# One kind of PSUM bank, eight reads: ScalarE's four ahead of VectorE's four in a neighbourhood attention

## The chip, the cores and the metric

One core of a Trainium2 chip. The metric is the device time of one execution in microseconds, smaller is better; of several runs the median is given. A difference below about 0.2% (5.5 us here) can hardly be told from none.

## What is computed

A trunk of two layers over 1024 latent tokens (a grid of 16 rows by 64 columns) and 256 context tokens, width 1024, 16 heads of 64. Layer 0 mixes tokens with a 2-D neighbourhood attention (window 8 x 16, learned bias) in which each latent query also sees all context keys; layer 1 with a sliding window. Both layers end in a gated ConvFFN. All is float32.

```python
def attn_inputs(h, w_qkv, g_q, g_k, n_kv, with_q=True):
    y = h @ w_qkv
    q = rmsnorm(y[..., :D_MODEL].reshape(bsz, t, n_kv, N_HEADS // n_kv, HEAD_DIM), g_q)
    kv = y[..., D_MODEL:]
    k = rmsnorm(kv[..., :kv_w].reshape(bsz, t, n_kv, HEAD_DIM), g_k)
    v = kv[..., kv_w:].reshape(bsz, t, n_kv, HEAD_DIM)
    return q, k, v
...
for i in range(DEPTH):
    h = modulate(rmsnorm(x, g_attn[i]), sh1, sc1)
    hc = modulate(rmsnorm(ctx, g_attn[i]), sh1c, sc1c)
    q, k, v = attn_inputs(h, w_in, gq, gk, n_kv)
    q_c, k_c, v_c = attn_inputs(hc, w_in, gq, gk, n_kv, with_q=not last)
    o = neighbourhood_attention(q, k, v, k_c, v_c, na_rpb[j])     # i = 0
    x = x + gt1 * (o @ w_out)
    ...                                                           # context alike, then ConvFFN
```

## The kernel before

The program runs its stages one after the other on one core: an opening (modulation vectors, norm and first projections), the first attention, its output projection, the ConvFFN of layer 0, and the same for layer 1. Within a stage a planner, `Sched`, makes the order: every operation is entered with an engine (or a choice of engines), an assumed duration, a key, what it reads and writes, and the buffer slots that it takes (`acq`) and gives back (`rel`). `run` plays the engines against those durations; among the operations that could start, the lowest key goes first. Tables of small corrections to the keys, `KINDS` (by the operation's name) and `RANKS` (by its number), belong to each stage. The result is a fixed order of instructions on each engine, and each engine executes in order. The waits between engines (semaphores) come from the tiles that instructions share, whole PSUM banks included, and not from the planner. Every instruction is recorded by one helper, so all stand under one line, L51; one goes by the tiles' names.

The first attention is the stage `na`. It goes over 8 pairs of heads (`hp`) and, for each, over 10 tiles of 128 tokens (the two of the context first) in `plan_na_qkv`: three products per 128 of depth into a bank `mm` (float32 is split into a high and a low part: `whi`/`wlo` are the weights', `h0hi`/`h0lo`, `n1lo`, `h0chi`/`h0clo` the activations'); ScalarE copies it out to `qraw`, squares it (`sq`); VectorE sums (`qv`); GpSimd takes the power -0.5 (`qy`); VectorE refines that and scales to `qn`. The value part `v` gets its low half by a subtraction on GpSimd or VectorE.

After every second tile comes **the turn**: four transposes (`pt<-idr,qn`) put queries and keys of two tiles, for both heads of the pair, into one bank `pt`: columns 0 to 255 are queries, 256 to 511 keys; head 0 lies in partitions 0 to 63, head 1 in 64 to 127. There are 40 turns. From this bank are made, for each of the two heads (`h2`), with names as the profile has them:

- `qh` (ScalarE, `q<-pt,gg`): the query's high part, scaled;
- `ql` (VectorE, `q<-pt,gg,q`): its low part, into the other half of the partitions;
- `kh` (ScalarE, `kkl<-pt`, for the context `kkc<-pt`): the key's high part;
- `kx` (`kkl<-kkl` or `kkc<-kkc`): a copy of it into the other half of the partitions, between SBUF and SBUF;
- `kl` (VectorE, `kll<-pt,kkl`, or `klc`): the key's low part.

So a bank sees eight reads, four by ScalarE and four by VectorE. The tag `pt` has two banks in rotation, and they serve every transpose of the stage: the turns, the transposed probabilities (`pt<-idr,S`, whose high part is ScalarE's `pthi<-pt` and whose remainder VectorE's `pthi<-pt,pthi`), and a few others (`pt<-wm,cpad`: modulation products; `pt<-idr,rs`: sums of the softmax). Whoever allocates a bank waits for the last read of the user before the last.

The scores (`s<-kkc,q`, `klc`, `kkl`, `kll`) and what follows are `plan_su`: VectorE makes the negated scores with the bias and their minimum (`S`, `m`), ScalarE the exponential, TensorE transposes, and the weighted sums go to `pv`; ScalarE and VectorE bring them out (`pvup`, `osb`). In the last two pairs of heads the probabilities are scaled (`S<-S,sm`) on VectorE or ScalarE; in the others the output is (`odiv`).

Of the kernel before, what the change touches and what calls it, by code (L numbers as in the profile page):

```python
# [12 lines left out]
F32R = mybir.dt.float32r  # L13
# [4 lines left out]
P = 128  # L18
# [20 lines left out]
class InOrder:  # L39
# [7 lines left out]
    def __getattr__(self, name):  # L47
        f = getattr(self.eng, name)

        def call(*a, **k):  # L50
# [11 lines left out]
    open=dict(load=-0.7, mm=-6.4, cp=0.6, tr=-3.7, fin_=-5.6, sq=4, v=-2.5, newton=4.7, dg=2.3, bc=0.5, lof=-10.6,  # L62
          mod=-1.6),
    na=dict(eps=-3.7, f=0.3, cp=-1, sq=-2.5, vhi=10, vlo=2.9, ql=-11.4, kl=0.1, mm=-0.1, ctx_part=5.2, exp=1.3, hi=-0.5,
          lo=0.5, pvm=-1.3, add=-11.1, load=-1, lat_part=-0.5, rec=3.4, ev=0.1, scale=9.4),
# [8 lines left out]
    open={0: 0.9, 1: 54.2, 3: 50.3, 4: 23, 5: 10.7, 7: 0.6, 9: -44.5, 10: -12.7, 12: -32.6, 13: 65.9, 14: 53,  # L74
# [17 lines left out]
    na={36: 1, 40: 28.4, 42: 3, 46: 15.2, 61: 3.8, 64: -25, 67: 12.6, 69: -45.3, 71: -43.5, 74: 12.7, 81: -34.3,  # L92
# [309 lines left out]
def trunk_kernel(ctx, tc, xperm, xtok, xseq, cc, wmod0, wmod, bmod, gnorm, na_wqkv, na_gq, na_gk, na_bias, na_wo,  # L402
# [124 lines left out]
    def t_actp(n):  # L527
        return 0.051 + n / 1200.0
# [816 lines left out]
    def plan_na_qkv(n):  # L1345
# [1797 lines left out]
```

## Time and profile before

| | us |
|---|---|
| median of 3 runs (lowest, highest) | 2764.96 (2764.88, 2765.37) |
| the profiled execution | 2765.64 |
| its span in the profile | 2763.9 |
| busy in the span: TensorE / VectorE / ScalarE / GpSimd | 2708.3 / 2272.7 / 1685.4 / 381.2 |
| granted TensorE clock, mean over the span | 0.998 |

TensorE is busy for 98% of the span, and the chain of work that ended last lies on it for 73%. An average over stages hides what one stage waits for: the first attention, from about 70 to 743 us, is the one that the change touches, and the opening ahead of it is planned with tables that also change. Busy time of TensorE counts modelled ends of matmuls, which overlap; two products one behind the other start closer together than either lasts. Idle time below 0.15 us is the pipeline's own and not listed as a wait.

### The profile page before, as it was taken

The page shows a single profiled execution, that of the slowest core. Times are in us where ns is not written, and L with a number is a line of the kernel's source. Part 1 is how long each engine was busy: PE and PEld are TensorE (multiplying, and loading weights), DVE is VectorE, ACT ScalarE, POOL GpSimd, SP SyncE. Part 2 cuts the span into 40 slices and gives each one's busy share as a digit, 9 for nine tenths or more (in the row PEclk, how much of TensorE's full clock was granted, in tenths as well). Part 3 has the DMA queues.
Part 4 walks back from the last instruction along what each step waited for, and adds up shares of the span by engine and source line. Part 5 has one row for each costly group of instructions (what it writes and reads, how often), then busy time and mean ns, then how long its engine had stood idle before and what let it go on. Part 6 is the DMA issues. An engine that isn't in the chain of part 4 may idle for free.

```text
span 2763.9 us, 43693 instructions
## 1 busy us (share of the span) xinstructions
PE 2708.3 (98%) x15375; PEld 2379.5 (86%) x15375; DVE 2272.7 (82%) x4767; ACT 1685.4 (61%) x3220; POOL 381.2 (14%) x631
## 2 busy tenths in 40 slices
PE   7999999999999999999999999999999999999999
PEld 6888898888789997788888889999988888888887
DVE  5777788889869677789998699888896989888766
ACT  5777676778646554455554457888874655555443
POOL 1211111113100000000000005556440000000000
PEclk9999999999999999999999999999999999999999
DMA  7223233333745654444467562010264234334745
GB/s 284 67 90 120 87 99 126 109 107 108 248 149 181 189 168 144 157 153 152 154 213 262 157 215 81 13 35 19 72 188 154 73 115 145 122 107 148 255 149 190
DMA packets 153104, 387.29 MB, mean 140 GB/s; under 512 B 23356, under 2 KB 38708, under 8 KB 151476
## 3 DMA queue, kind: packets, MB, share of 16 engines
q1 hardware_dynamic: 152884, 384.50, 42.3%
q8 instruction: 121, 1.98, 0.3%
q14 instruction: 99, 0.81, 0.1%
HBM read 313.39 MB, written 71.04 MB: 139 GB/s over the span
## 4 chain that ended last, share of the span: by engine, by line
PE 73%; DVE 2%; ACT 2%; DMA 1%; issue 1%; POOL 0%; SPq 0%; DVEq 0%; POOLq 0%; ACTq 0%
PE ua L51 17%; PE dn L51 15%; PE uc L51 12%; PE mm L51 8%; PE ud L51 4%; PE oacc L51 4%; PE pt L51 3%; PE pv L51 3%; PE s L51 3%; PE dnc L51 2%; PE u L51 1%; ACT S L51 0%; PE mod L51 0%; ACT whi L51 0%; DVE S L51 0%
## 5 line engine op out<-in xcount | busy, mean ns | idle before, releaser
L51 ACT ACTIVATE whi<-wraw 128x512 fp32r<-128x512 f32 (+1 forms) x264 | 213.0, 808 | 180.8 <-PE uc L51 55.4
L51 DVE TENSOR_TENSOR wlo<-wraw,whi 128x512 fp32r<-128x512 f32 (+1 forms) x264 | 240.8, 914 | 39.9 <-ACT whi L51 39.4
L51 ACT ACTIVATE S<-S,m 128x640 f32<-128x640 f32 (+4 forms) x288 | 220.9, 768 | 50.3 <-DVE m L51 43.6
L51 PE MATMUL dn<-ghi,whi 128*128 128x512 f32 x616 | 239.9, 390 | 0.0
L51 PE MATMUL dn<-ghi,wlo 128*128 128x512 f32 x616 | 239.7, 389 | 0.0
L51 PE MATMUL dn<-glo,whi 128*128 128x512 f32 x616 | 239.6, 389 | 0.0
L51 ACT ACTIVATE pthi<-pt 128x512 fp32r<-128x512 f32 (+2 forms) x384 | 195.8, 522 | 67.5 <-PE pt L51 35.1
L51 DVE SCALAR_TENSOR_TENSOR u<-c,cv,u 128x1023 f32<-128x1023 f32 x176 | 222.3, 1280 | 3.3 <-ACT u L51 2.8
L51 PE MATMUL pt<-idr,S 128*128 128x128 f32 x1280 | 196.4, 274 | 22.3 <-DVE kll L51 11.0
L51 ACT ACTIVATE whi<-s 128x1024 fp32r<-128x1024 f32 (+1 forms) x116 | 109.0, 940 | 164.9 <-PE uc L51 105.6
L51 ACT ACTIVATE ghi<-graw 128x512 fp32r<-128x512 f32 x154 | 96.5, 631 | 175.8 <-PE dn L51 101.7
L51 PEld LDWEIGHTS pt<-idr,S 128*128 128x128 f32 x1280 | 150.8, 140 | 42.8 <-issue 15.0
L51 PE MATMUL mm<-whi,h0hi 128*128 128x384 f32 x480 | 168.8, 352 | 0.0
L51 DVE TENSOR_TENSOR glo<-graw,ghi 128x512 fp32r<-128x512 f32 x154 | 105.8, 691 | 74.7 <-ACT ghi L51 68.8
L51 PE MATMUL mm<-wlo,h0hi 128*128 128x384 f32 x480 | 161.4, 336 | 0.0
L51 PE MATMUL pv<-pthi,v 128*128 128x256 f32 (+1 forms) x560 | 152.0, 353 | 5.8 <-DVE osb L51 3.2
L51 POOL TENSOR_TENSOR qy<-qv,mhalf 128x4 f32<-128x4 f32 (+1 forms) x112 | 122.3, 1093 | 190.2 <-DVE qv L51 159.4
L51 DVE TENSOR_TENSOR wlo<-s,whi 128x1024 fp32r<-128x1024 f32 (+1 forms) x116 | 124.5, 1076 | 22.8 <-ACT whi L51 22.6
L51 DVE TENSOR_TENSOR pthi<-pt,pthi 128x512 fp32r<-128x512 f32 (+2 forms) x208 | 118.4, 582 | 27.2 <-ACT pthi L51 25.8
L51 PEld LDWEIGHTS dn<-glo,whi 128*128 128x128 f32 x616 | 115.6, 188 | 24.1
L51 PEld LDWEIGHTS dn<-ghi,whi 128*128 128x128 f32 x616 | 115.6, 188 | 24.0
L51 PEld LDWEIGHTS dn<-ghi,wlo 128*128 128x128 f32 x616 | 115.6, 188 | 23.9
(405 smaller groups left out, 8522.8 us busy)
## 6 DMA issues: line engine op xcount, KB each, us to landing
wraw<-in_w_up_dram SPq DMA_DIRECT2D x132, 512.0 KB, 3.9
wm<-in_wmod_dram SPq DMA_DIRECT2D x80, 512.0 KB, 3.8
wraw<-in_w_down_dram SPq DMA_DIRECT2D x44, 512.0 KB, 4.2
graw<-g_dram SPq DMA_DIRECT2D x44, 512.0 KB, 4.5
wraw<-in_w_down_dram SPq DMA_DIRECT2D x88, 256.0 KB, 3.0
graw<-g_dram SPq DMA_DIRECT2D x66, 256.0 KB, 2.8
slab<-in_na_wqkv_dram SPq DMA_DIRECT2D x32, 384.0 KB, 3.3
woraw<-in_na_wo_dram SPq DMA_DIRECT2D x24, 512.0 KB, 4.8
```

What stands on the lines that cost most here:

```text
L51: r = f(*a, **k)
```

## The change

In `plan_na_qkv`, for each turn:

- the four VectorE operations (`ql`, `kl` for both heads) are entered after the four ScalarE ones and read all four of their results (`whole`), so that the planner starts them only when ScalarE is done with the bank; they are collected in `late`;
- `qh` and `kh` no longer read each other's results; `qh` is assumed to take 0.09 us more;
- `kx`, before on ScalarE or GpSimd as the planner chose, is on GpSimd, assumed at 0.5 us;
- the slots for the new tiles of queries and context keys are taken by the transposes `tr` instead of by the readers, and for the latent keys `tr` is entered as a writer (`olds`) of the places that the turn will overwrite, so that it comes after their last use.

The tables `KINDS` and `RANKS` of the stages `open` and `na` are new; by them the opening and the whole first attention, up to the output projection at 743 us, stand in another order. From there on the order on every engine is the same.

```diff
-    na=dict(eps=-3.7, f=0.3, cp=-1, sq=-2.5, vhi=10, vlo=2.9, ql=-11.4, kl=0.1, mm=-0.1, ctx_part=5.2, exp=1.3, hi=-0.5,
+    na=dict(eps=-1.8, cp=3.1, sq=-2.8, pw=-5.5, vhi=4.8, vlo=2.4, qn=-3.6, kh=-3.7, kx=3.7, ql=-5.9, mm=-0.1, qkc=0.3,
...
         def tr(e):
             pt = J["pt"] = psa("pt", F32)
+            f["q"][pr] = fin.tile([P, 2, 2 * P], F32R, tag="qc" if cx else "q", name="q", bufs=1 if cx else 4)
+            if cx:
+                f["kkc"] = fin.tile([P, 2, TC], F32R, tag="kkc", name="kkc", bufs=2)
...
-        sc.op("pe", 0.436, tr, reads=[K("qn"), before + ("qn",)], writes=[K("pt")], key=key, acq=[("pt", K("pt"), 8)],
+        slots = [("qc", q, 4), ("kkc", ("kkc", hp), 20), ("klc", ("klc", hp), 20)] if cx else [("q", q, 8)]
+        olds = [] if cx else [(y, pr, h2) for y in ("kh", "kx", "kl") for h2 in range(2)]
+        sc.op("pe", 0.436, tr, reads=[K("qn"), before + ("qn",)], writes=[K("pt")] + olds, key=key, acq=[("pt", K("pt"), 8)] + slots,
                rel=[K("qn"), before + ("qn",)])
+        late = []
...
-            sc.op("act", t_actp(256), qh, reads=[K("pt")] + [q + ("h", 0)] * h2, writes=[q + ("h", h2)], key=key,
-                  acq=[] if h2 else [("qc", q, 4) if cx else ("q", q, 8)], rel=[K("pt")])
+            sc.op("act", t_actp(256) + 0.09, qh, reads=[K("pt")], writes=[q + ("h", h2)], key=key, rel=[K("pt")])
...
-            sc.op("dve", t_dve(256) + 0.06, ql, reads=[K("pt"), q + ("h", h2)], writes=[q + ("l", h2)], key=key, rel=[K("pt")],
-                  port=False)
+            late.append((t_dve(256) + 0.06, ql, dict(reads=[K("pt"), q + ("h", h2)], writes=[q + ("l", h2)], rel=[K("pt")])))
...
-            sc.op("act", t_actp(256), kh, reads=[K("pt")] + [kt("kh", 0)] * (h2 and cx), writes=[kt("kh", h2)], key=key,
-                  acq=[("kkc", ("kkc", hp), 20)] if cx and h2 == 0 else (), rel=[K("pt")])
+            sc.op("act", t_actp(256), kh, reads=[K("pt")], writes=[kt("kh", h2)], key=key, rel=[K("pt")])
...
-            sc.op(("act", "pool"), (t_act(256), t_pool(256)), kx, reads=[kt("kh", h2)], writes=[kt("kx", h2)], key=key)
+            sc.op("pool", 0.5, kx, reads=[kt("kh", h2)], writes=[kt("kx", h2)], key=key)
...
-            sc.op("dve", t_dve(256), kl, reads=[K("pt"), kt("kh", h2), kz], writes=[kt("kl", h2)], key=key,
-                  acq=[("klc", ("klc", hp), 20)] if cx and h2 == 0 else (), rel=[K("pt")], port=False)
+            late.append((t_dve(256), kl, dict(reads=[K("pt"), kt("kh", h2), kz], writes=[kt("kl", h2)], rel=[K("pt")])))
+        whole = [q + ("h", h2) for h2 in range(2)] + [kt("kh", h2) for h2 in range(2)]
+        for t, fn, k in late:
+            sc.op("dve", t, fn, reads=k.pop("reads") + whole, key=key, port=False, **k)
```

Three places of the new order, all at the 23rd of the 40 turns (fifth pair of heads, latent tiles 2 and 3; in the profile before at 401 us). First TensorE. Before, from the turn's transposes to the next allocation of the same bank, which is the last row (`pt<-wm,cpad` takes the other bank):

```order
L51 MATMUL pt<-idr,qn 128x128 x4
L51 MATMUL mm<-whi,h0hi_135 128x384
L51 MATMUL mm<-whi,n1lo 128x384
L51 MATMUL mm<-wlo,h0hi_135 128x384
L51 MATMUL mm<-whi,h0hi_135 128x384
L51 MATMUL mm<-whi,n1lo 128x384
L51 MATMUL mm<-wlo,h0hi_135 128x384
L51 MATMUL pv<-pthi,v 128x512 x2
L51 MATMUL pt<-wm,cpad 32x256 x8
L51 MATMUL pt<-idr,rs_4093 20x128
```

Now, from the same turn's transposes on:

```order
L51 MATMUL pt<-idr,qn 128x128 x4
L51 MATMUL mm<-whi,h0hi_135 128x384
L51 MATMUL mm<-whi,n1lo 128x384
L51 MATMUL mm<-wlo,h0hi_135 128x384
L51 MATMUL mm<-whi,h0hi_135 128x384
L51 MATMUL mm<-whi,n1lo 128x384
L51 MATMUL mm<-wlo,h0hi_135 128x384
L51 MATMUL pt<-wm,cpad 32x256 x8
L51 MATMUL s<-kkc,q 128x256
L51 MATMUL s<-klc_697,q 128x256
L51 MATMUL s<-kkc,q 128x256
L51 MATMUL s<-klc_697,q 128x256
```

Where the next user of the bank stood, there are now scores of the pair of heads before; behind them follow more scores and nine more products `mm`, and the bank is allocated again only after those.

Second ScalarE at this turn (the bank is `pt_5200` before, `pt_5131` now). Before:

```order
L51 ACTIVATE q_5210<-pt_5200,gg_692 64x256
L51 ACTIVATE kkl_694<-pt_5200 64x256
L51 ACTIVATE q_5210<-pt_5200,gg_692 64x256
L51 ACTIVATE kkl_694<-kkl_694 64x256
L51 ACTIVATE kkl_694<-pt_5200 64x256
L51 ACTIVATE qraw_5234<-mm_5135 128x384
L51 ACTIVATE kkl_694<-kkl_694 64x256
```

Now:

```order
L51 ACTIVATE pvup_5129<-pv_5100 64x256
L51 ACTIVATE kkl_694<-pt_5131 64x256 x2
L51 ACTIVATE q_5132<-pt_5131,gg_692 64x256 x2
L51 ACTIVATE qraw_5161<-mm_5072 128x384
L51 ACTIVATE sq0_698<-qraw_5161 128x4x64
```

The four reads stand together, the keys' first, and the two copies `kkl<-kkl` have left this engine. Over the stage 58 + 13 of them move to GpSimd.

Third GpSimd, where these copies now stand (the first pair here belongs to the turn ahead, the second to this one):

```order
L51 CAST kkl_694<-kkl_694 64x256 x2
L51 TENSOR_TENSOR qy_5103<-qv_5097,mhalf_98 128x4
L51 CAST kkl_694<-kkl_694 64x256 x2
L51 TENSOR_TENSOR v_5173<-qraw_5161,v_5173 128x2x64
L51 TENSOR_TENSOR qy_5199<-qv_5188,mhalf_98 128x4
L51 TENSOR_TENSOR qy_5303<-qv_5292,mhalf_98 128x4
```

Before, this stretch of GpSimd's queue held only powers `qy` and subtractions `v`; 9 copies stood there in the whole stage, now 80.

More of the change, by code (lines that the diff above doesn't have):

```diff
@@ L61 @@
 KINDS = dict(
[L62 to L65 removed]
+    open=dict(load=-0.8, mm=-4, tr=-3.1, fin_=-10.1, sq=6.9, v=4.1, dg=9, bc=-6.7, lof=-4.6, mod=-1.1),
+    na=dict(eps=-1.8, cp=3.1, sq=-2.8, pw=-5.5, vhi=4.8, vlo=2.4, qn=-3.6, kh=-3.7, kx=3.7, ql=-5.9, mm=-0.1, qkc=0.3,
+          ctx_part=3.7, exp=-1.3, hi=-0.5, lo=0.5, pvm=-3.7, up=-2.4, add=-0.2, load=-0.7, lat_part=-0.5, rec=2.4,
+          ev=-9.2, scale=9.1, fin_=-10.1),
     ffn0=dict(),
@@ L1411, in qh @@
             def qh(e, h2=h2, r=r):
-                if h2 == 0:
-                    f["q"][pr] = fin.tile([P, 2, 2 * P], F32R, tag="qc" if cx else "q", name="q", bufs=1 if cx else 4)
                 act.activation(f["q"][pr][r, h2, :], J["pt"][r, 0:256], AF.Copy, scale=gg[r, :])
-            sc.op("act", t_actp(256), qh, reads=[K("pt")] + [q + ("h", 0)] * h2, writes=[q + ("h", h2)], key=key,
-                  acq=[] if h2 else [("qc", q, 4) if cx else ("q", q, 8)], rel=[K("pt")])
+            sc.op("act", t_actp(256) + 0.09, qh, reads=[K("pt")], writes=[q + ("h", h2)], key=key, rel=[K("pt")])
             def ql(e, h2=h2, r=r, x=x):
@@ L1421, in ql @@
                                          op0=ALU.mult, op1=ALU.subtract)
-            sc.op("dve", t_dve(256) + 0.06, ql, reads=[K("pt"), q + ("h", h2)], writes=[q + ("l", h2)], key=key, rel=[K("pt")],
-                  port=False)
+            late.append((t_dve(256) + 0.06, ql, dict(reads=[K("pt"), q + ("h", h2)], writes=[q + ("l", h2)], rel=[K("pt")])))
             def kh(e, h2=h2, r=r):
-                if cx and h2 == 0:
-                    f["kkc"] = fin.tile([P, 2, TC], F32R, tag="kkc", name="kkc", bufs=2)
                 copy(e, kh_t()[r, h2, pair_cols], J["pt"][r, 256:512])
-            sc.op("act", t_actp(256), kh, reads=[K("pt")] + [kt("kh", 0)] * (h2 and cx), writes=[kt("kh", h2)], key=key,
-                  acq=[("kkc", ("kkc", hp), 20)] if cx and h2 == 0 else (), rel=[K("pt")])
+            sc.op("act", t_actp(256), kh, reads=[K("pt")], writes=[kt("kh", h2)], key=key, rel=[K("pt")])
             def kx(e, h2=h2, r=r, x=x):
                 copy(e, kh_t()[x, h2, pair_cols], kh_t()[r, h2, pair_cols].bitcast(F32))
-            sc.op(("act", "pool"), (t_act(256), t_pool(256)), kx, reads=[kt("kh", h2)], writes=[kt("kx", h2)], key=key)
+            sc.op("pool", 0.5, kx, reads=[kt("kh", h2)], writes=[kt("kx", h2)], key=key)
             def kl(e, h2=h2, r=r):
```

4 lines of the change are left out of this document (2 added, 2 removed), and 225 rows, old and new, of tables (na, open).

## The prediction

> **What bounds the kernel now.** I read the stages first, with the busy time of each engine in four stretches: the opening, the first attention, its tail, and all that follows. The columns are the length, the busy time (and count) of TensorE, its weight loads, VectorE, ScalarE and GpSimd, then the granted clock, the DMA share and GB/s.
>
> ```profile
> core 0: us, PE busy (x) PEld busy (x) DVE busy (x) ACT busy (x) POOL busy (x), PEclk, DMA share, GB/s
> 0.00:70.00 70.00, 54.52 (x384) 47.19 (x385) 40.83 (x119) 41.75 (x76) 9.53 (x18) 0.93 0.75 281
> 70.00:680.00 610.00, 582.10 (x3781) 536.53 (x3779) 492.32 (x1585) 443.72 (x1086) 118.82 (x148) 1.00 0.31 100
> 680.00:743.00 63.00, 57.94 (x350) 49.14 (x350) 50.01 (x123) 43.00 (x86) 15.85 (x13) 1.00 0.68 230
> 743.00:2764.00 2021.00, 2013.76 (x10866) 1746.65 (x10864) 1689.54 (x2943) 1156.92 (x1973) 236.96 (x452) 1.00 0.44 145
> ```
>
> From 743 us on TensorE is busy for 2013.76 of 2021 us, and the change leaves the order there as it was. So the whole question lies in the first 743 us, and most of it in the 610 us of the first attention: TensorE is idle there for 610 - 582.1 = 27.9 us, VectorE for 118 and ScalarE for 166. TensorE is the bound, and a time won must be one of its waits. Second, therefore, what TensorE waited for from 70 to 743 us (total us, times, longest):
>
> ```profile
> PE pt L51 <- DVE kll L51: 12.9, 16, 1.3
> PE pt L51 <- DVE klc L51: 3.7, 4, 1.2
> PE pt L51 <- DVE pthi L51: 3.4, 7, 1.0
> PE pv L51 <- DVE osb L51: 3.2, 4, 1.1
> PE pt L51 <- ACT S L51: 2.9, 3, 1.5
> PE pv L51 <- DVE pthi L51: 2.1, 6, 0.7
> PE pt L51 <- DVE qn L51: 0.8, 2, 0.5
> ```
>
> Three of the rows are one thing: a transpose that wants a "pt" bank stands until VectorE's last read (kll, klc or q) of the bank that holds turned queries and keys. They come to 12.9 + 3.7 + 0.7 = 17.3 us in 21 waits. All other rows shown sum to 3.4 + 3.2 + 2.9 + 2.1 = 11.6 us. Third, one such turn as the timeline tells it (start, length, instruction, idle time before it):
>
> ```profile
> 401.06 0.60 PE L51 MATMUL pt<-idr,qn 128*128 128x128 f32 x4
> ...
> 401.70 0.47 ACT L51 ACTIVATE q<-pt,gg 64x256 fp32r<-64x256 f32 x1 [0.89 <-PE pt L51]
> 401.85 0.34 PE L51 MATMUL mm<-wlo,h0hi 128*128 128x384 f32 x1
> ...
> 402.02 0.34 PE L51 MATMUL mm<-whi,h0hi 128*128 128x384 f32 x1
> ...
> 402.07 0.37 ACT L51 ACTIVATE kkl<-pt 64x256 fp32r<-64x256 f32 x1
> ...
> 402.46 0.47 ACT L51 ACTIVATE q<-pt,gg 64x256 fp32r<-64x256 f32 x1
> ...
> 402.96 0.48 DVE L51 SCALAR_TENSOR_TENSOR q<-pt,gg,q 64x256 fp32r<-64x256 f32 x1 [1.18 <-PE pv L51]
> ...
> 403.10 1.07 PE L51 MATMUL pt<-wm,cpad 128*32 128x256 f32 x16
> 403.45 0.42 DVE L51 TENSOR_TENSOR kll<-pt,kkl 64x256 fp32r<-64x256 f32 x1
> ...
> 403.90 0.38 ACT L51 ACTIVATE kkl<-pt 64x256 fp32r<-64x256 f32 x1 [0.53 <-DVE kll L51]
> ...
> 404.31 0.49 DVE L51 SCALAR_TENSOR_TENSOR q<-pt,gg,q 64x256 fp32r<-64x256 f32 x1 [0.44 <-ACT kkl L51]
> 404.82 0.43 DVE L51 TENSOR_TENSOR kll<-pt,kkl 64x256 fp32r<-64x256 f32 x1
> ...
> 405.39 0.27 PE L51 MATMUL pt<-idr,rs 128*20 128x128 f32 x1 [1.22 <-DVE kll L51]
> ```
>
> The four transposes start at 401.06; eight reads empty the bank, four by ScalarE (two q, two kkl) and four by VectorE (two q, two kll). They never overlap: ScalarE's second kkl starts 0.03 us after VectorE's kll has ended, and VectorE's second q 0.03 us after that kkl. The last read ends at 405.25, 4.19 us after the first transpose, and the next user of this bank starts at 405.39, after TensorE has stood for 1.22 us. What TensorE had in its queue in between was too little.
>
> **The reads in a new order.** The prices come from the stage's groups by form (busy us, mean ns, idle before):
>
> ```profile
> L51 DVE SCALAR_TENSOR_TENSOR q<-pt,gg,q 64x256 fp32r<-64x256 f32 x80 | 38.7, 483 | 46.8 <-ACT q L51 28.1 <-ACT kkl L51 10.3 <-PE pv L51 4.9
> ...
> L51 ACT ACTIVATE q<-pt,gg 64x256 fp32r<-64x256 f32 x80 | 37.4, 467 | 16.5 <-PE pt L51 14.5 <-DVE kll L51 0.5
> ...
> L51 DVE TENSOR_TENSOR kll<-pt,kkl 64x256 fp32r<-64x256 f32 x64 | 27.0, 422 | 10.4 <-ACT q L51 7.1 <-ACT kkl L51 2.4
> ...
> L51 ACT ACTIVATE kkl<-kkl 64x256 fp32r<-64x256 f32 x58 | 24.1, 415 | 1.3
> L51 ACT ACTIVATE kkl<-pt 64x256 fp32r<-64x256 f32 x64 | 23.8, 372 | 15.0 <-PE pt L51 6.9 <-DVE kll L51 5.3 <-DVE q L51 1.9
> ...
> L51 POOL TENSOR_TENSOR qy<-qv,mhalf 128x4 f32<-128x4 f32 x78 | 80.8, 1037 | 157.0 <-DVE qv L51 126.4 <-ACT S L51 8.9 <-DVE sm L51 8.0
> ...
> L51 ACT ACTIVATE S<-S,sm 128x640 f32<-128x640 f32 x11 | 9.1, 824 | 0.7 <-DVE sm L51 0.7
> ...
> L51 DVE TENSOR_SCALAR S<-S,sm 128x640 f32<-128x640 f32 x13 | 7.3, 564 | 0.1
> ...
> L51 DVE TENSOR_TENSOR v<-qraw,v 128x128 fp32r<-128x128 f32 x21 | 5.9, 283 | 2.3 <-ACT v L51 2.3
> ...
> L51 ACT ACTIVATE kkc<-kkc 64x256 fp32r<-64x256 f32 x13 | 5.4, 417 | 0.3
> ...
> L51 POOL CAST kkl<-kkl 64x256 fp32r<-64x256 f32 x6 | 2.9, 481 | 21.8 <-ACT kkl L51 21.8
> ```
>
> After the change ScalarE's four reads come first, 2 x 467 + 2 x 372 = 1.68 us, and VectorE's four follow, 2 x 483 + 2 x 422 = 1.81 us. With the 0.64 us from the first transpose to the first read and about 0.05 us at the handover, the bank is held for 0.64 + 1.68 + 0.05 + 1.81 = 4.18 us. That is the 4.19 us of the turn above: the reads exclude each other in either order, so fewer handovers by themselves buy next to nothing. I price this part at 0.
>
> The row shows that a read of the lower half of the partitions by VectorE (kll, 403.45) holds back a read of the upper half by ScalarE (kkl, 403.90, idle 0.53 us). The Trainium skill ("PSUM — Partial Sum Buffer", section "PSUM bank collisions raise a hardware error") says that two engines must be kept apart only where they touch the same bank and the same group of 32 partitions, reads against reads included. By that rule the old order could read two halves at once, the bank would be free about 0.9 us sooner than under the new order, and the change would cost up to 40 x 0.9 = 36 us where TensorE waits for it; the sum by the row is 0. This case's trace decides for the row: the program waits by whole bank, so there is no overlap to lose.
>
> **What TensorE has to do meanwhile.** The timeline's two products at 401.85 and 402.02 start 0.17 us apart for 384 columns; in proportion to columns I estimate 0.12 us for 256, 0.23 for 512 and 0.06 for a transpose of 128, and the sixteen 32-row products take 1.07 us together. With these I counted, for each of the 40 turns, TensorE's work from the first transpose to the next allocation of the same bank (the second one after, since there are two). Before, it is less than 4.2 us in 29 of 40 turns, and what is missing sums to 26.3 us; the trace has 17.3 us of waits for it, 0.66 of that. After, 11 turns are short, none below 3.6 us (23 before), and 2.4 us are missing in sum. The turn above goes from 2.8 to 7.5 us of work. This is where the gain is.
>
> At the same ratio the remaining wait is 2.4 x 0.66 = 1.6 us. That is the lower end: it holds only if nothing else stands between the reads. In the new order 21 turns have one or two other ScalarE instructions among the four reads and 16 have some of VectorE's. Added with their durations the missing time is about 12 us, so 12 x 0.66 = 7.9 us of waits is the upper end. I take 4.0, nearer to the lower one, as most of these turns miss only a few tenths. Gain: 17.3 - 4.0 = 13.3 us (9.4 to 15.7).
>
> **The copies on GpSimd.** 58 + 13 copies leave ScalarE: 71 x 415 ns = 29.5 us, off the path, since ScalarE has 166 us idle in the stage. On GpSimd they take 71 x 481 ns = 34 us; it is busy for 118.8 of 610. In the queue each pair stands among the v subtractions and the powers qy (1037 ns), and waits for ScalarE's kkl reads. In 31 of 40 turns the two kkl reads come first; the copies can start 0.05 + 0.75 us after ScalarE's first read began and need 2 x 0.48 us, with a power ahead 1.04 more: 2.8 us, still ahead of VectorE's last read, which ends at 1.68 + 0.05 + 1.81 = 3.5. So the score products, which need both, are not later: cost 0. If that cover were gone, each turn would pay up to 1.04 us, but only where the scores follow at once; the shortest distance from a turn to its first score product is 3.6 us of TensorE work after, and was 2.6 before. The power behind a copy may be 0.96 us later; it leads over VectorE to the qn of a later turn, and in 4 of 76 tiles that path has under 5.7 us of TensorE's work above it (10 before): below 2 us, taken as 0.
>
> One row of the trace, for the copies' spread (min/median/max):
>
> ```profile
> L51 POOL CAST kkl<-kkl x6: 391/396/912, 193.5 to 679.2; 64x256 fp32r<-64x256 f32 x6
> ```
>
> The worst copy took 912 ns instead of 396. The Trainium skill ("SBUF — State Buffer", section "SBUF: two separate sides") has GpSimd and VectorE share one pair of ports, held for a whole instruction, when VectorE has two operands in SBUF; 71 more copies would then be 71 chances to block each other. By that rule at worst 71 x 0.48 = 34 us go to VectorE's idle 118 us, so the sum is the same by it; the maximum above is what the trace has in its favour.
>
> **What moves with them.** Nine softmax scalings go from ScalarE to VectorE (564 ns instead of 824 for 640 columns), nine v subtractions from GpSimd to VectorE at 283 ns, while six other subtractions and products leave it: VectorE gains about 3 us net, of 118 idle. ScalarE, 37 us lighter, answers TensorE sooner at S (2.9 us of waits): a gain of 0 to 2.9. Against it, work drawn into the turns (5.4 us on average, 4.1 before) is missing elsewhere, so pthi and osb waits may grow; bounded by 0 and a doubling, 8.7. By the count of work between other transposes the shortage there rises by a tenth, so 1 us. I set both to 1; they cancel. The slots' allocation at the turn adds no instruction; it keeps TensorE from filling a bank whose readers cannot start yet (cost 0 to the few tenths in 11 turns, already in the upper end above). The opening is reordered in its tables without a count of TensorE's instructions changing: 0, bounds -2 and +2 of its 15.5 us idle. SP's queue has the same 1088 entries, in another order; no row shown waits for a DMA.
>
> Sum: 13.3 + 1 - 1 = 13.3 us. The profiled execution took 2765.64 us (span 2763.9), 0.7 above the median of the runs; against it the sum gives 2752.3, and the same 13.3 off the median of 2764.96 gives **2751.7**.
>
> **Rivals.**
> - *The stall only moves.* TensorE executes in order and its work is unchanged; 40 x 1.3 = 52 us of it is drawn into the turns and no longer covers weighted sums and other transposes. If their 11.6 us of waits double, 13.3 - 11.6 = 1.7 us are left: 2763.3. For it: 95% of the stage is already busy, so slack is thin. Against it: counted the same way, the distances between the other transposes hardly shorten (3.39 to 3.32 us on average).
> - *Slower: VectorE becomes the bound at its first late read.* It now waits for all four of ScalarE's reads; behind it, in order, stand the score minima and the pthi remainders, for which the exponentials and the sums wait. Today it idles 46.8 + 10.4 = 57 us before q and kll, 1.4 us a turn. With 495 us of work it becomes the bound when 495 + 40w passes 597, at w = 2.55 us a turn. If nothing stands ahead of it, w is 0.64 + 1.68 + 0.05 and one other ScalarE instruction of about 0.7, 3.07: 495 + 123 = 618 instead of 610 us in the stage, so 2773. Against it: in the turn above VectorE's first read would start at 403.43 instead of 402.96, only 0.5 us later, which makes w 1.9.
> - *More than forecast.* All but 1.6 us of the 17.3 go, the S waits vanish (2.9), and the opening gains 2: 20.6 us, 2744.4.
>
> **How the numbers follow.** Faster as forecast (2744 to 2759) has 0.78, since the count of work explains today's waits turn by turn; a stall that only moves 0.13; VectorE as the bound 0.07; more than 21 us 0.02. A difference under 0.2% (5.5 us) is about what a measurement cannot tell from none. Faster by more is then 0.80, the same 0.13, slower 0.07. The range reaches from the lower end of the forecast, 2743, to the moved stall, 2763.
>
> **What would show it.** Right: the waits of pt for kll, klc and q fall from 17.3 us to 2 to 8, TensorE's busy time in the stage stays at 582 while the stage ends 11 to 15 us earlier, a bank is still held for about 4.2 us, and ScalarE's kkl to kkl copies are gone, with GpSimd's at 0.4 to 0.5 us. Wrong: these waits fall, but pthi and osb rise by as much (first rival); or VectorE's idle time before q and kll passes 2.5 us a turn (second); or the bank's hold grows beyond 5 us because of instructions between the reads.

## The result: 26 us, twice the forecast

| | before | changed kernel |
|---|---|---|
| median (lowest, highest), us | 2765.16 (2764.88, 2765.37), 4 runs | 2739.1 (2738.3, 2743.53), 4 runs |
| ratio, 95% interval | | 0.9909 [0.9892, 0.9926] |
| span of the profiled execution, us | 2763.9 | 2737.5 |

The forecast was 2751.7 us, from 2743 to 2763: the direction was right, the gain is 26.1 us instead of 13.3, and the time lies below the range. The stages of the changed kernel, cut where the same work ends (columns as in the prediction):

```profile
core 0: us, PE busy (x) PEld busy (x) DVE busy (x) ACT busy (x) POOL busy (x), PEclk, DMA share, GB/s
0.00:70.00 70.00, 53.45 (x395) 46.47 (x396) 42.77 (x126) 42.64 (x80) 9.56 (x18) 0.98 0.76 281
70.00:655.00 585.00, 576.56 (x3757) 533.62 (x3756) 490.58 (x1588) 411.01 (x1002) 146.92 (x216) 1.00 0.33 103
655.00:717.00 62.00, 58.66 (x363) 51.26 (x363) 52.20 (x127) 42.26 (x85) 16.46 (x12) 1.00 0.75 250
717.00:2737.50 2020.50, 2013.17 (x10866) 1746.34 (x10865) 1687.37 (x2943) 1157.70 (x1973) 237.35 (x452) 1.00 0.44 144
```

The last row has the same 10866 matmuls in 2020.5 us as before in 2021.0: the time is gained ahead of it. I divide by two marks instead of fixed times. From the first turn to the first weight load of the ConvFFN (70.66 to 811.43 us before, 68.92 to 785.47 now) the stretch shrank from 740.8 to 716.6 us, 24.2 of the 26.4 us between the spans, with the same 4435 matmuls. What TensorE waited for from 70 to 717 us:

```profile
PE pt L51 <- DVE kll L51: 1.4, 4, 0.6
PE mm L51 <- ACT qraw L51: 1.4, 1, 1.4
PE pv L51 <- DVE osb L51: 1.3, 3, 0.6
PE s L51 <- DVE m L51: 1.3, 3, 0.7
PE pt L51 <- DVE pthi L51: 1.1, 3, 0.5
PE pv L51 <- DVE pthi L51: 1.1, 4, 0.4
...
PE pt L51 <- DVE klc L51: 0.4, 1, 0.4
```

All rows of this view sum to 10.7 us; before, from 70 to 743, to 31.7. The turns' waits (kll, klc, q) went from 17.3 to 1.8, the two pthi rows from 5.5 to 2.2, the rest from 8.9 to 6.7. A stop costs TensorE more than the idle time shown: a product of 384 columns lasts 0.34 us in the profile and the next usually starts 0.17 us after it, but idle time is counted only from the modelled end, so the lost overlap comes on top. Counted from the start of one matmul to that of the next, less the usual distance for its shape, the stops of the stretch (those with over 0.15 us of idle time) cost 40.5 us before and 15.4 now. That is 25.1, and no other term is needed for the 24.2.

The 23rd turn (for its instructions before, see the prediction):

```profile
382.29 0.60 PE L51 MATMUL pt<-idr,qn 128*128 128x128 f32 x4
...
382.92 0.78 ACT L51 ACTIVATE kkl<-pt 64x256 fp32r<-64x256 f32 x2 [0.58 <-PE pt L51]
...
383.43 0.85 POOL L51 CAST kkl<-kkl 64x256 fp32r<-64x256 f32 x2 [2.58 <-ACT kkl L51]
...
383.73 0.95 ACT L51 ACTIVATE q<-pt,gg 64x256 fp32r<-64x256 f32 x2
...
384.71 0.42 DVE L51 TENSOR_TENSOR kll<-pt,kkl 64x256 fp32r<-64x256 f32 x1 [1.47 <-ACT q L51]
...
385.14 0.98 DVE L51 SCALAR_TENSOR_TENSOR q<-pt,gg,q 64x256 fp32r<-64x256 f32 x2
...
386.14 0.43 DVE L51 TENSOR_TENSOR kll<-pt,kkl 64x256 fp32r<-64x256 f32 x1
...
390.46 0.34 PE L51 MATMUL mm<-wlo,h0hi 128*128 128x384 f32 x1
390.64 0.82 PE L51 MATMUL pt<-idr,S 128*128 128x128 f32 x6
```

The hold is 386.57 - 382.29 = 4.28 us, as long as before; the next user of the bank comes at 390.64 and waits for nothing. Over all 40 turns the banks are held *longer* than before: 5.12 us in the mean (median 4.77) against 4.68 (4.34). What became shorter is VectorE's idle time ahead of its reads. Its groups, from 68 to 700 us:

```profile
L51 DVE SCALAR_TENSOR_TENSOR q<-pt,gg,q 64x256 fp32r<-64x256 f32 x80 | 38.7, 483 | 18.5 <-ACT q L51 13.3 <-ACT kkl L51 1.8 <-ACT kkc L51 1.7
...
L51 DVE TENSOR_TENSOR kll<-pt,kkl 64x256 fp32r<-64x256 f32 x64 | 27.0, 421 | 2.5 <-ACT q L51 1.5
```

46.8 + 10.4 us before are 18.5 + 2.5 now. (The third group, klc, makes it 57.9 and 21.2 in the table further below.) VectorE executes in order; while it stands for ScalarE at a turn, the remainders of the probabilities (pthi) and the score minima behind it stand too.

### The profile page after: what moved, and what is told of

Its sections match the earlier page's. It is cut to its first block, busy times and chain, and to the rows that moved or that the text cites. A ratio compares the mean times of both kernels' runs of the same rounds, so it can differ in the third digit from the quotient of the medians.

```text
span 2737.5 us, 43801 instructions
## 1 busy us (share of the span) xinstructions
PE 2701.8 (99%) x15375; PEld 2377.7 (87%) x15375; DVE 2272.9 (83%) x4782; ACT 1653.6 (60%) x3138; POOL 410.3 (15%) x698
## 3 DMA queue, kind: packets, MB, share of 16 engines
q1 hardware_dynamic: 152884, 384.50, 43.1%
## 4 chain that ended last, share of the span: by engine, by line
PE 72%; DVE 2%; ACT 1%; DMA 1%; issue 0%; POOL 0%; SPq 0%; DVEq 0%; ACTq 0%
PE ua L51 17%; PE dn L51 15%; PE uc L51 13%; PE mm L51 6%; PE oacc L51 5%; PE ud L51 4%; PE pt L51 3%; PE pv L51 3%; PE s L51 2%; PE dnc L51 2%; PE u L51 2%; PE mod L51 0%; DVE wlo L51 0%; DVE S L51 0%; DVE pthi L51 0%
## 5 line engine op out<-in xcount | busy, mean ns | idle before, releaser
L51 ACT ACTIVATE S<-S,m 128x640 f32<-128x640 f32 (+3 forms) x288 | 220.9, 768 | 58.8 <-DVE m L51 50.0
L51 ACT ACTIVATE pthi<-pt 128x512 fp32r<-128x512 f32 (+2 forms) x384 | 196.1, 523 | 73.1 <-PE pt L51 40.9
L51 POOL TENSOR_TENSOR n1y<-n1v,mhalf 128x4 f32<-128x4 f32 (+1 forms) x8 | 8.9, 1108 | 907.3 <-DVE n1v L51 907.3
L51 DVE TENSOR_TENSOR wlo<-s,whi 128x1024 fp32r<-128x1024 f32 (+1 forms) x116 | 124.4, 1075 | 22.5 <-ACT whi L51 22.2
```

Of the source, the lines that this page charges most:

```text
L51: r = f(*a, **k)
```

## The experiments

The prediction's steps give a theory, *cover*: work of TensorE behind each turn is the gain; the order of the reads and GpSimd's copies are worth nothing by themselves. The rivals are its zeros: the order of the reads, ScalarE's queue, and the order of everything else. "Missing work" below is what the turns lack against 4.15 us of TensorE's work, at the prediction's prices (it used 4.2, hence 24.9 us before instead of 26.3). All differences are against the kernel before on the same chip (medians of 2765.2 to 2767.5 us). The code of each experiment is abridged: words and `...` in it stand for longer code.

### One part at a time, the rest of the order kept

*b_cover.* Before's order, with the only edit that free products `mm` are drawn ahead of a bank's next allocation until a turn has 4.3 us of TensorE's work by the planner's durations:

```diff
+for a, b, c in zip(banks, banks[1:], banks[2:]):   # a: a turn's bank, c: its next allocation
+    while work(a, c) < 4.3: move the next free mm product to just before c
```

> The kernel before, with one edit of TensorE's order: where TensorE has less than 4.3 us of work between a turn and the next allocation of the same bank, the next free mm products are drawn ahead of that allocation (the missing work sums to 2.9 us instead of 26.3). Reads, engines and tables stay as before. Theory (what counts is the work that stands behind a turn): the waits of pt for kll, klc and q fall from 17.3 to about 3 us, and the time by 12 to 17 us, to 2748 to 2753; the rest of the change's 26 us lies elsewhere in the new order. Rival (the grouped reads or the copies on GpSimd make the gain): no change, 2762 to 2768. Rival (the stall only moves): turn waits fall, other waits of TensorE rise by as much, 2760 to 2765.

Measured: 2763.59 us, 0.9989 [0.998, 0.9999], 2.8 us. Its waits (70 to 745 us):

```profile
PE pv L51 <- DVE pthi L51: 6.8, 13, 1.2
PE pt L51 <- DVE pthi L51: 5.9, 9, 1.1
...
PE pt L51 <- DVE klc L51: 2.2, 2, 1.6
PE pt L51 <- DVE kll L51: 0.9, 3, 0.4
```

The turns' waits fell as counted, to 3.1 us, and the pthi rows rose from 5.5 to 12.7. Cover alone mostly moves the stall: for this order the prediction's first rival was right.

*b_group.* Before's order, only ScalarE's four reads issued ahead of VectorE's four, in all 40 turns (39 of them alternate before):

```diff
-qh0 kh0 qh1 ql0 kl0 kx0 kh1 kx1 ql1 kl1    # before: the reads stand so in 11 of 40 turns, the commonest order
+qh0 kh0 qh1 kh1 kx0 kx1 ql0 kl0 ql1 kl1
```

> The kernel before, with its own order on TensorE; only at each of the 40 turns ScalarE's four reads are issued ahead of VectorE's four, in the places that the ten instructions of the turn already had. Theory: the reads exclude each other in either order, a bank is still held for 4.1 to 4.3 us, and the time stays within 3 us of before. Rival (the grouped reads make the gain): at least 8 us faster, 2757 or less.

Measured: 2767.64 us, 1.0007 [0.9997, 1.0016]. In this order the reads' sequence is worth nothing, as priced.

*a_alt.* The opposite in the changed kernel: its order, with the reads alternating again.

> The changed kernel with its own plan; only at each turn the ten instructions are issued in the older pattern (ScalarE q, key, q, VectorE q, key, ScalarE key, VectorE q, key). Theory: the work behind the turns is unchanged, so the time stays within 3 us of the changed kernel, 2736 to 2743. Rival (the grouped reads make the gain): 8 us or more of the 26 are lost, 2747 or more.

Measured: 2750.37 us, 0.9947 [0.9932, 0.9962]; 10 of the 26 us are lost, and my expectation with them. TensorE's order is the same, the turns still lack only 1.8 us and wait 2.3. The row for VectorE's read:

```profile
L51 DVE SCALAR_TENSOR_TENSOR q<-pt,gg,q 64x256 fp32r<-64x256 f32 x80 | 38.7, 483 | 43.1 <-ACT q L51 32.8 <-ACT kkl L51 5.8 <-PE s L51 2.4
```

43.1 us of idle time instead of 18.5. So where the turns are covered, the sequence of reads does count. VectorE's queue is not the only one that stands longer: ScalarE, whose second key read waits for VectorE again, idles 24.6 us ahead of its reads of the turned banks (groups q, kkl, kkc) instead of 12.6. Which of the two makes the 10 us is not parted here.

*a_act.* The changed kernel's order, the 80 copies issued by ScalarE at the places where GpSimd had them:

```diff
-on[kx] = "pool"
+on[kx] = "act"
```

> The changed kernel with its own plan; only the 80 copies of the keys' high parts are issued on ScalarE instead of GpSimd, in the same places. Theory: ScalarE has over 150 us idle in the stage and the copies cost it 33 us off the path: within 4 us of the changed kernel, 2737 to 2743. Rival (ScalarE's relief makes much of the gain): 8 us or more are lost, 2747 or more.

Measured: 2764.66 us, 0.9997 [0.9987, 1.0006]: nearly the whole gain is lost, and my price of 0 with it. A turn shows how:

```profile
388.50 0.60 PE L51 MATMUL pt<-idr,qn 128*128 128x128 f32 x4
...
389.13 0.78 ACT L51 ACTIVATE kkl<-pt 64x256 fp32r<-64x256 f32 x2 [1.61 <-PE pt L51]
...
389.94 0.39 ACT L51 ACTIVATE pthi<-pt 128x256 fp32r<-128x256 f32 x1
...
390.35 0.42 ACT L51 ACTIVATE kkl<-kkl 64x256 fp32r<-64x256 f32 x1
...
390.78 0.47 ACT L51 ACTIVATE q<-pt,gg 64x256 fp32r<-64x256 f32 x1
...
391.26 0.42 ACT L51 ACTIVATE kkl<-kkl 64x256 fp32r<-64x256 f32 x1
...
391.69 0.47 ACT L51 ACTIVATE q<-pt,gg 64x256 fp32r<-64x256 f32 x1
...
392.19 0.98 DVE L51 SCALAR_TENSOR_TENSOR q<-pt,gg,q 64x256 fp32r<-64x256 f32 x2 [1.41 <-ACT q L51]
...
393.19 0.86 DVE L51 TENSOR_TENSOR kll<-pt,kkl 64x256 fp32r<-64x256 f32 x2
...
394.19 0.63 PE L51 MATMUL pt<-idr,S 128*128 128x128 f32 x4 [0.85 <-DVE kll L51]
```

Each copy stands ahead of one of ScalarE's own reads of the bank (390.35 ahead of 390.78, 391.26 ahead of 391.69; over all turns 48 of the 80 copies stand between such reads), VectorE's first read comes after 1.41 us of idling, and TensorE waits 0.85 us for the last. Over all turns the banks are held 5.66 us, VectorE idles 40.5 us ahead of its reads, and the turns' waits are back at 10.3 us.

*a_defer1.* Is it the place of the copies or the work? The same copies on ScalarE, but behind all its reads of the bank and at least one more instruction:

```diff
-# on ScalarE, a_act:  kkl<-pt x2, q<-pt, kkl<-kkl, q<-pt, kkl<-kkl, others ...
+# a_defer1:            kkl<-pt x2, q<-pt x2, one or more others, kkl<-kkl x2, ...
```

> The changed kernel with its 80 key copies on ScalarE, but issued later than there: behind all of ScalarE's reads of the bank and one or more other instructions, instead of between and right behind its reads. The same copies at the places of GpSimd's gave 2764.7 us, with the banks held 5.66 us in the mean instead of 5.12. Theory P (the place in ScalarE's queue: the copies delay the reads of the bank and the hand-over to VectorE): 2742 to 2752 us, the banks held 5.0 to 5.3 us. Theory O (occupancy: 80 times 415 ns, 33 us more on an engine on which every eviction and exponential behind them comes later): 2758 to 2766 us wherever the copies stand, with the waits of TensorE moved from kll to pthi, S and osb.

Measured: 2750.03 us, 0.9936 [0.9921, 0.9951], holds 5.12 us, VectorE's idle time ahead of its reads 21.3. Of the 24 us that a_act lost, the place in the queue made 15. The other 9 stay lost with the copies on ScalarE; whether by its time or because the later copies reach the score products later is not parted.

*a_dve.* The copies on VectorE at the same places of the order (`on[kx] = "dve"`):

> The changed kernel with its 80 key copies issued by VectorE instead of GpSimd, at the same places of the order. Theory R (what counts is that ScalarE is rid of them): 2738 to 2747 us; VectorE has some 70 us idle in this stage and the copies take 20 to 35 us of it. Theory V (VectorE is as tight, since q's second reads, the subtractions of P's halves and the scores' maxima all stand on it): 2752 to 2768 us, with TensorE's idle time between first and last turn at 18 us or more and VectorE's waits shorter than after's.

Measured: 2747.62 us, 0.993 [0.9915, 0.9945], just above theory R's range: VectorE needs only 289 ns for a copy (ScalarE 416, GpSimd 396, medians), and still 80 of them cost 6.5 us against GpSimd.

*b_pool and b_pc.* Before's order with the copies on GpSimd, without and with b_cover's edit.

> Before's code and before's order of all the work; only the 71 key copies that ScalarE issued in the first attention are issued by GpSimd (all 80 of them then are). Known by now: the changed kernel with its copies put back on ScalarE loses 24 of its 26 us. Theory A (relief): a copy on ScalarE of 415 ns stands ahead of the next reads and evictions there, and taking 71 of them away brings TensorE's operands earlier in any order of the work; then most of the gain is here too: 2742 to 2752 us, TensorE's idle time from the first turn to the last down from 27.0 us to 10-15. Theory B (both are needed): the relief is worth something only where TensorE also has work behind each turn, which this order lacks in 29 of 40 turns: 2757 to 2764 us, the idle time 20-26, and waits for kll, klc and q still 10 us or more. Theory C (the order fits its engine): each order suits the engine that its copies were placed for, and any other assignment loses: 2765 us or more.

> Before's code with two edits: the key copies on GpSimd, as above, and free products of the projection drawn ahead so that each turn has at least 4.3 us of TensorE's work behind it until the bank's next allocation. The second edit alone gave 2763.6 us. Theory A (relief adds to whatever cover there is): 2738 to 2748 us, the copies' share 15 to 20 us and the cover's some 3. Theory B (both are needed, and together they are the change): 2738 to 2748 us too, but far below both single edits: the two gains together exceed the sum of the single ones by over 8 us. Theory C (the order fits its engine): above 2758 us.

Measured: 2766.71 us, 0.9998 [0.9989, 1.0008], and 2763.17 us, 0.9982 [0.9973, 0.9992]. In before's order the relief of ScalarE is worth nothing, with cover or without, as priced, though 36 copies stand between ScalarE's reads there too. Both times lie in theory C's ranges, but nothing is lost either, as that theory has it. None of these parts brings the gain in before's order; the order itself had to be looked at.

### Rules or tables

The order comes from the planner's rules and from tables. b0 and a0 have the first attention's tables empty; x_bt has the change's rules with before's tables, x_at the reverse. (x_bt and the four cases further below have the changed kernel's opening too; in twelve profiles with that opening the first turn stood at 70.1 us in the mean, 68.2 to 72.0, in eight with before's at 71.2, 70.1 to 71.9: about 1 us.)

```diff
-sc.rank(RANKS["na"], KINDS["na"])
+sc.rank({}, {})          # b0, a0; x_bt and x_at: the other kernel's two tables, numbers mapped within a turn
```

> Before's code with the first attention's two tables of numbers empty, so that the planner's own rules set the order there. Together with the next run this parts what the rules do from what the tables do. By the order, the 40 turns then lack 29.6 us of TensorE's work behind them until the bank's next allocation (24.9 with the tables, by the same count). All theories expect a time above before's: 2775 to 2830 us. Theory R (rules): the next kernel, with the change's rules and no tables either, is at least 10 us faster than this one. Theory T (tables): the two differ by less than 6 us or the other way round.

> The changed kernel with the first attention's two tables empty. The turns then lack 5.9 us of TensorE's work (1.8 with the tables). Theory R (the change's rules, that is all ScalarE's reads first, the slots taken by the turn and the copies on GpSimd, make the order that covers the turns): at least 10 us below the run without tables before it, and the turns' waits in the trace below 8 us. Theory T (the new tables make it): within 6 us of that run, or slower.

> The changed code with before's tables for the first attention (the numbers of the operations inside each turn mapped to their new places). The turns lack 3.4 us. Theory R: the rules carry the gain, 2740 to 2753 us. Theory T: the gain is of the new numbers, 2757 to 2775 us. Theory F (numbers and rules fit only each other): above 2765 us, as well as the run below.

> Before's code with the changed kernel's tables for the first attention (numbers mapped the other way). The turns lack 16.8 us, against 24.9 with before's tables and 1.8 in the changed kernel. Theory R: 2757 to 2770 us, no better than before by more than 8 us. Theory T: 2738 to 2750 us. Theory F: above 2765 us.

Measured: b0 2771.15 us, 1.0013 [1.0004, 1.0022]; a0 2749.55, 0.9937 [0.9922, 0.9952]; x_bt 2741.8, 0.9911 [0.9894, 0.9927]; x_at 2777.53, 1.0037 [1.0022, 1.0052]. The rules bring 21.6 us without tables and 25.1 with before's; the new tables by themselves, in before's rules, lose 10.7. The rules carry the gain (theory R), though b0 came out below, and x_at above, the times expected of them.

### Which rule

Four cases, before's tables, laid out anew: r1000 has the reads rule alone (VectorE's reads depend on all of ScalarE's), r0010 the copies on GpSimd alone, r1010 both, r0110 copies and slots.

```diff
+sc.op("dve", t, fn, reads=k.pop("reads") + whole, ...)      # r1000, r1010
+sc.op("pool", 0.5, kx, ...)                                 # r0010, r1010, r0110
+..., acq=[("pt", K("pt"), 8)] + slots                       # r0110
```

> Before's code and tables with one rule of the change alone: each of VectorE's four reads of a turned bank is made to depend on all four of ScalarE's, and the planner lays out the order anew. The copies stay with ScalarE or GpSimd by the planner's choice, the slots are taken as before. The planner then counts a bank held for 4.41 us in the mean (before 3.40, the changed kernel 4.51, on the chip 4.34 in the median before). The turns lack 1.9 us of work (before 25.1). Theory H (the gain is that the plan counts the bank's real hold, and the reads rule does that): 2740 to 2750 us. Theory P (GpSimd's copies are needed, since ScalarE's put back cost 24 us in the changed kernel): 2752 to 2765 us.

> The other two rules without the reads rule, in before's code and tables, planned anew: the slots taken by the turn, the copies on GpSimd at 0.5 us. The turns lack 22.8 us, nearly as before. Theory H: 2757 to 2770 us. Theory P (relief of ScalarE in a plan made for it): 2740 to 2753 us.

> Before's code and tables with the key copies on GpSimd at a price of 0.5 us as the only rule of the change, and the order laid out anew (in an earlier run the copies alone were moved, in before's own order, and nothing changed). The turns lack 22.8 us of work. Theory J (the reads rule makes the order, and the copies then keep ScalarE's queue short enough for it; neither does the other's part): 2757 to 2775 us. Theory S (the 10 us lost with slots and copies together were the slots'): below 2757 us.

> Before's code and tables with two rules, the reads rule and the copies on GpSimd, without the slots taken by the turn. With the reads rule alone 2754.8 us were measured, with all three in these tables 2741.8. The turns lack 6.5 us. Theory J: 2738 to 2748 us, the two rules together worth over 8 us more than the sum of each alone. Theory S (the slots matter as well): 2750 to 2760 us.

Measured: r1000 2754.76 us, 0.9955 [0.9941, 0.997]; r0110 2777.43, 1.0038 [1.0025, 1.0051]; r0010 2774.06, 1.0024 [1.0013, 1.0035]; r1010 2748.99, 0.9937 [0.9921, 0.9954]. Against before that is -12.7 for the reads rule, +6.5 for the copies, +10.0 for copies and slots (above both of its ranges), -18.5 for reads rule and copies, -25.1 for all (x_bt). r1000 misses theory H's range, and r1010 is 1 us above theory J's, but the two rules together are 12.3 us better than the sum of each alone, as it has it: the copies on GpSimd pay only in an order that the reads rule made. What slots and the 0.09 us on qh add, 6.5 us, lies by the estimate below for the most part in TensorE's clock and not in its waits.

*b_hold12.* The reads rule makes the planner count a bank as held 4.41 us in the mean, where before it counted 3.40 and the chip took a median of 4.34. Is that all it does? Here before's planner counts a turn's bank free 1.2 us later, and nothing else is changed. *a_hold06* adds 0.6 us to the change's count.

```diff
-x[2] = max(x[2], end[i] + 0.18)
+x[2] = max(x[2], end[i] + 0.18 + (1.2 if turn_read(o) and tag == "pt" else 0.0))     # a_hold06: 0.6
```

> Before's kernel with one number of the planner changed: a bank of a turn is counted free 1.2 us later than before. No read is regrouped and no copy moved by a rule; the planner lays out the order anew. The turns lack 1.0 us of work. Theory H: most of the gain without any of the change's rules, 2740 to 2753 us, TensorE's idle time from first to last turn 8 to 14 us instead of 27.0. Theory G (the grouped reads themselves are needed in such an order: undone in the changed kernel they cost 10 us): 2750 to 2758 us. If it is above 2758 us, the hold that the planner counts isn't the cause.

> The changed kernel with a turn's bank counted free 0.6 us later, nearer to the 5.12 us that the chip holds it there in the mean (the plan: 4.51). The turns lack nothing then (1.8 before this edit). Theory H: 2736 to 2741 us, since only 1.8 us of the turns' waits are left to take and the tables were made for the other count; over 2745 us would say that the order's other waits come back as soon as it is laid out anew.

Measured: 2765.23 us, 0.9994 [0.9984, 1.0003], and 2758.24, 0.9966 [0.9954, 0.9979]. Both expectations of theory H missed, theory G's too, and b_hold12 lies above the 2758 us from which on the counted hold isn't the cause. In b_hold12 (70 to 745 us):

```profile
PE pv L51 <- DVE pthi L51: 15.8, 20, 2.0
PE pt L51 <- DVE pthi L51: 6.5, 10, 1.5
```

No wait of a turn is left, and the pthi rows stand at 22.3 us (5.5 before): all of it moved. Like b_cover it has the cover without the rest. VectorE still idles 48.8 us ahead of its reads there, in r1000, where the cover is about the same, 26.0.

### All kernels side by side

Missing work of the turns (count of the order), VectorE's idle time ahead of its reads of turned banks (groups q, kll, klc, 68 to 700 us), cost of TensorE's stops from the first turn to the first product of the ConvFFN (from start to start), the time for which TensorE was granted half of its clock in that stretch, and the difference from before, all in us; the last column is of medians, the others of one profiled execution each:

| kernel | missing | VectorE idle | stops | at half clock | against before |
|---|---|---|---|---|---|
| before | 24.9 | 57.9 | 40.5 | 0 | |
| b_group | 24.9 | 41.0 | 40.4 | 0 | +1.3 |
| b_pool | 24.9 | 56.8 | 40.5 | 0 | -0.5 |
| b0 | 29.6 | 58.1 | 40.9 | 3.4 | +4.3 |
| x_at | 16.8 | 56.2 | 50.0 | 3.4 | +10.7 |
| r0010 | 22.8 | 53.4 | 45.4 | 6.8 | +6.5 |
| r0110 | 22.8 | 55.0 | 45.5 | 6.8 | +10.0 |
| b_cover | 2.9 | 57.5 | 32.6 | 0 | -2.8 |
| b_pc | 2.9 | 56.7 | 34.0 | 0 | -4.0 |
| b_hold12 | 1.0 | 48.8 | 39.3 | 3.4 | -2.2 |
| a_act | 1.8 | 40.5 | 35.3 | 3.4 | -1.7 |
| a_alt | 1.8 | 44.1 | 25.4 | 0 | -16.0 |
| r1000 | 1.9 | 26.0 | 22.3 | 13.6 | -12.7 |
| a_hold06 | 0.0 | 17.9 | 24.9 | 20.4 | -9.2 |
| r1010 | 6.5 | 26.8 | 17.9 | 10.2 | -18.5 |
| a_defer1 | 1.8 | 21.3 | 19.1 | 0 | -17.2 |
| a_dve | 1.8 | 9.2 | 22.5 | 0 | -19.6 |
| a0 | 5.9 | 18.1 | 18.3 | 6.8 | -17.3 |
| x_bt | 3.4 | 25.4 | 16.6 | 0 | -25.1 |
| changed kernel | 1.8 | 21.2 | 15.4 | 0 | -26.1 |

No kernel without cover gains more than 0.5 us. Of those with cover and VectorE still idling 40 us or more ahead of its reads, three gain 2 to 4 us, a_act 1.7, and only a_alt 16: that one keeps the changed kernel's order of everything else, so VectorE's idle time is not the whole of it. All those with both gain 9 to 26. The reads rule brings both: the bank's next use is placed later, and VectorE's reads are placed behind ScalarE's, with other work of VectorE ahead of them.

The 16 us between the other layouts made with the reads rule (2741.8 to 2758.2) are for the most part other stops and TensorE's clock. The same stretch in a_hold06 and in the changed kernel (columns as above; the third number from the end is the granted clock):

```profile
649.00:718.00 69.00, 56.86 (x344) 50.52 (x343) 56.97 (x140) 45.56 (x92) 15.35 (x14) 0.85 0.49 153
649.00:718.00 69.00, 65.29 (x409) 57.10 (x408) 58.15 (x144) 48.80 (x100) 19.11 (x15) 1.00 0.72 239
```

In a_hold06's stretches of half clock products of 256 columns start 0.21 us apart instead of 0.12, so I estimate that 0.43 of the time at half clock is lost: 9 us in a_hold06, 6 in r1000, 4 in r1010, 3 in a0. With 9.5 us of further stops that is about the 17 us by which a_hold06, with nothing missing at its turns, falls short of the changed kernel. Between r1010 and x_bt the stops differ by only 1.3 us.

Shown is that under before's rules neither half suffices alone (b_group; b_cover, b_hold12), that the reads rule alone brings about half of the gain and the copies on GpSimd add to it (r1000, r1010), and, with TensorE's order held, what the sequence of reads (a_alt) and the copies' place (a_act against a_defer1) are worth. Open: b_group's and b_cover's edits together in before's order weren't run, so whether the two do it without a new layout is argued only. No version was faster than the changed kernel.

## Why the prediction was half right

What failed is the pair of prices of 0, for the order of the reads and for relieving ScalarE of the copies; with them the forecast left out that the other waits fall as well. In the terms of the sum the 26.1 us are 15.5 for the turns' waits (forecast 13.3), 5.5 for all other waits (forecast 0 net), 4.1 for what stops cost beyond their idle time (left out) and about 1 for the opening (forecast 0). That the direction was right is in part luck, since the term that carried it nets 2.8 us by itself in before's order.

- **Work behind the turns** (the term of 13.3 us). The waits for kll, klc and q fell by 15.5 us, inside its 9.4 to 15.7. But it was read as a net gain, and in before's order the same cover nets 2.8 (b_cover). The count names the waits that go; whether others take their place was left to a rival at 0.13, and to the term below. The count's price of 0.06 us for a transpose was also too low: in the turn shown with the prediction four take 0.60 us, and one lasts 0.27, so they start 0.11 us apart. The 26.3 us of missing work were thus counted too high.
- **What moves with them** (+1 and -1). This term failed. I let pthi and osb waits grow by 1 us, because cover is taken from elsewhere; all waits other than the turns' (14.4 us, of which I summed 11.6) fell to 8.9. With the 15.5 this makes 21.0 us of idle time, and 25.1 counted from start to start, which my sum, made in idle time, left out.
- **The reads, priced 0** because the hold stays 4.2 us. Right in before's order (b_group), wrong in the new one, where it is worth 10 us (a_alt). The price was looked for in the bank's hold; it lay in the queues of the engines that read, where others' work stands behind the reads. My second rival saw that queue, but with the opposite sign: idle time ahead of q and kll is 0.5 us a turn now, not 1.9 to 3.07, and was 1.4 before.
- **The copies, priced 0** "since ScalarE has 166 us idle in the stage". The step that failed most: 0 in before's order (b_pool), 24 us in the new one (a_act), 15 of them for standing ahead of ScalarE's own reads. Idle time over a stage is no cover for an instruction that stands ahead of a late one. On GpSimd the copies went as priced: 396 ns, and the longest took 587, though 71 more shared the stage with VectorE:

```profile
L51 POOL CAST kkl<-kkl x64: 392/396/587, 76.7 to 654.6; 64x256 fp32r<-64x256 f32 x64
```

The Trainium skill ("SBUF — State Buffer", section "SBUF: two separate sides") has GpSimd and VectorE block each other at a shared pair of ports when VectorE reads two operands from SBUF. With 64 of these copies the median is what it was with 6, so no cost of that shows in them.
- **The sign for failure** that I named, a hold beyond 5 us, came true (5.12) while the time fell: a long hold costs little once the turn has work behind it (1.8 us of waits). TensorE's busy time of 582 us for the stage could not settle anything, since it counts modelled ends; the stops from start to start could.
- **The opening** (0, ±2): 1.7 us between the two profiles, about 1 over twenty.

## What to carry to other kernels

When a stall of an in-order engine is to be filled, count what fills it *and* what is then missing elsewhere, in the waiting engine's own queue first: cover alone brought 3 us here, cover with VectorE's late reads moved behind its other work 9 to 26. An engine's idle share says nothing of an instruction's price; look at what stands right behind it in its queue and who waits for that. And where a planner makes the order, check the durations that it counts against the trace (3.40 us counted, 4.34 taken), but expect a new layout to move other waits too (9.5 us in a_hold06), and look at the granted clock before a difference between two layouts is put down to their waits.

## What was not expected of the hardware

A copy of 64x256 floats from SBUF to SBUF takes VectorE 289 ns, GpSimd 396 and ScalarE 416 (medians of 64), so GpSimd was not the slowest place for it. A stop of TensorE costs more than the idle time that the profile shows: before, 48 stops with 31.9 us of it cost 40.5 from start to start, now 25 with 10.7 cost 15.4, some 0.18 us more for each, about the 0.17 us by which two products of 384 columns usually overlap in the profile.

TensorE's granted clock fell to half for 3.4 or 6.8 us where TensorE had idled much. The profiles of all these kernels have 18 such stretches between the first turn and the ConvFFN, and in the 6.8 us ahead of each one TensorE had idled for 1.9 us or more in sum (r1000: one stop of 3.5 us, then half clock from 652.1 to 658.9). Not every such stop is followed by one: in a_hold06 one of 2.4 us at 98 us is not. Before and the changed kernel have no stop over 1.5 us there and stay at full clock.
